# A channel MLP's block products computed as seven instead of eight in the second layer

## The chip, the cores and the metric

The kernel runs on one core of one Trainium2 chip. The metric is the device time of one execution in microseconds (us); the median of three runs is given, with their lowest and highest. Times in the sections below come from one profiled execution.

## What is computed

Two layers of a diffusion trunk over 640 tokens: 512 latent ones and 128 context ones, of width 1024. Each layer mixes the tokens by three branches, projects the merged result, and ends with a squared-ReLU MLP of hidden width 4096, which is where the change acts. Everything is held in fp32.

```python
def layer(x, cond, lp, lam_init, cached):
    ...
    merged = g_a * (y_a @ lp['w_o_gla']) + g_b * (y_b @ lp['w_o_mla']) + g_c * (y_c @ lp['w_o_diff'])
    x = x + gt1 * (merged @ lp['w_out'])

    h2 = rms_norm(x, lp['g_norm2']) * (1 + sc2) + sh2
    x = x + gt2 * (jnp.square(jax.nn.relu(h2 @ lp['w_mlp1'])) @ lp['w_mlp2'])
    return x, new_state
```

Layers are numbered 0 and 1. "Layer one" is the second and last.

## The kernel before

**Products.** TensorE multiplies 128x128 weight tiles with 256 or 384 token columns, since the tokens are cut into HALVES of 256 and 384. Every fp32 operand is split into a high part, which ScalarE makes by a cast (L98, or L1329 for the hidden values), and a low part, which is the operand minus its high part and comes from VectorE (L100, L1331). A product is then three matmuls for each 128 rows of the contraction: high by high, high by low, low by high (mm3, L105 to L107). At the start of the kernel and in parts of layer 0 GpSimd makes the low parts of weights in VectorE's place.

**The MLP.** The hidden width is cut into four blocks j of 1024. A block has 8 weight tiles of w1 (up) and then 8 of w2 (down); each tile is 128 columns of output by 1024 of contraction, 512 KB. load_w fetches a tile in one DMA issued by SyncE, casts it and subtracts, in turn with buffers of tag w (wraw 2, whi and wlo 3 each) and of tag x (xraw 1, xhi and xlo 3 each). A tile costs TensorE 8 x 3 matmuls of 256 columns and 8 x 3 of 384. An up tile's result goes through ReLU and square on ScalarE (L1328, L1329); GpSimd squares the ReLU once more in fp32 (L1330) for the low part. A down tile's result is scaled and added into the residual x by VectorE, straight from PSUM (L1279).

**Ahead of it.** out_proj (L1289) multiplies the merged rows by w_out for both token halves, adds them into x, and gathers sums of squares on ScalarE (L282) and VectorE (L283). norm (L330 to L334) turns x into the MLP's input: statistics matmuls (L301), a chain of twelve small VectorE instructions for 1/sqrt (L127 to L134), a broadcast matmul (L305), and then for each of the 8 tiles of 128 rows a product (VectorE, "nt"), the high part with the shift added (ScalarE, "hh") and the low part (VectorE, "hl"). The first half is normed while out_proj still works on the second.

**Order.** Each engine has its own queue, worked off in order. A list scheduler in the framework orders the instructions of each queue; a buffer's next use waits until its last reader is done. DMAs of weights are issued by SyncE in order.

**Rope tables.** The rope table (384 KB) is loaded once at the start and stays in SBUF; tables(l) at L338 works out per-layer tables from it on GpSimd (L363, L371).

## Time and profile before

| | |
|---|---|
| median of three runs | 2612.6 us (2611.7 to 2614.41) |
| the profiled execution's own time | 2612.42 us |
| its span, first to last instruction | 2610.6 us |
| first matmul of layer 1's MLP | 2155.79 us |
| last matmul of all | 2606.22 us |

The span starts at the first instruction. Busy time is the time in which an engine executes; a wait is put down to what ended it. "Granted clock" 1.00 is TensorE's higher level of 2.4 GHz and 0.50 its lower of 1.2 GHz.

### The profile page before, as it was taken

The page shows a single profiled execution, that of the slowest core. Times are in us where ns is not written, and L with a number is a line of the kernel's source. Part 1 is how long each engine was busy: PE and PEld are TensorE (multiplying, and loading weights), DVE is VectorE, ACT ScalarE, POOL GpSimd, SP SyncE. Part 2 cuts the span into 40 slices and gives each one's busy share as a digit, 9 for nine tenths or more (in the row PEclk, how much of TensorE's full clock was granted, in tenths as well). Part 3 has the DMA queues.
Part 4 walks back from the last instruction along what each step waited for, and adds up shares of the span by engine and source line. Part 5 has one row for each costly group of instructions (what it writes and reads, how often), then busy time and mean ns, then how long its engine had stood idle before and what let it go on. Part 6 is the DMA issues. An engine that isn't in the chain of part 4 may idle for free.

```text
span 2610.6 us, 45018 instructions
## 1 busy us (share of the span) xinstructions
PE 2511.1 (96%) x17616; PEld 2428.3 (93%) x17616; DVE 1595.3 (61%) x3613; ACT 1195.1 (46%) x2358; POOL 407.6 (16%) x550
## 2 busy tenths in 40 slices
PE   7899999899899999999989999998999999999999
PEld 3898999898899999999989888998989999999999
DVE  5787666578564776666655776666764455333332
ACT  4376687466333423132335777765652334132230
POOL 1321233010020111020221222511002001011010
PEclk9999999999999999999989999999999999999999
DMA  7411111413653244444421111123225332222221
GB/s 264 166 52 66 54 51 56 122 52 126 214 162 133 88 162 153 153 150 149 137 72 54 47 58 64 43 74 94 82 89 181 134 108 89 73 73 79 75 74 49
DMA packets 107572, 269.22 MB, mean 103 GB/s; under 512 B 12064, under 2 KB 42016, under 8 KB 105824
## 3 DMA queue, kind: packets, MB, share of 16 engines
q1 hardware_dynamic: 107360, 266.34, 30.6%
q8 instruction: 139, 2.28, 0.4%
q14 instruction: 73, 0.60, 0.1%
HBM read 235.86 MB, written 30.44 MB: 102 GB/s over the span
## 4 chain that ended last, share of the span: by engine, by line
PE 78%; DVE 12%; ACT 5%; DMA 3%; issue 2%; POOL 1%; SPq 0%; DVEq 0%; ACTq 0%; POOLq 0%
PE g L105 19%; PE g L106 19%; PE g L107 19%; PE go L534 2%; PE f L105 2%; PE f L106 2%; PE f L107 2%; DVE mjunk L212 1%; DVE sm_m L784 1%; PE y L1056 1%; PE g L852 1%; DMA modwe<-wmod 1%; DVE wlo L100 1%; PE gt L107 1%; PE gt L105 1%
## 5 line engine op out<-in xcount | busy, mean ns | idle before, releaser
L98 ACT CAST whi<-wraw 128x1024 fp32r<-128x1024 f32 (+2 forms) x236 | 220.2, 933 | 446.1 <-PE g L106 385.9
L100 DVE TENSOR_TENSOR wlo<-wraw,whi 128x1024 fp32r<-128x1024 f32 (+3 forms) x230 | 252.3, 1097 | 228.6 <-ACT whi L98 221.5
L105 PE MATMUL g<-hh,whi 128*128 128x256 f32 (+1 forms) x992 | 311.9, 314 | 6.5 <-DVE gla_t L633 4.8
L107 PE MATMUL g<-hh,wlo 128*128 128x256 f32 (+1 forms) x992 | 310.5, 313 | 3.3 <-DVE wlo L100 3.3
L106 PE MATMUL g<-hl,whi 128*128 128x256 f32 (+1 forms) x992 | 309.8, 312 | 0.0
L1330 POOL TENSOR_TENSOR relu<-relu 128x256 f32<-128x256 f32 (+1 forms) x128 | 110.8, 866 | 940.8 <-ACT uh L1329 937.9
L1279 DVE SCALAR_TENSOR_TENSOR x<-g,moda,x 128x256 f32<-128x256 f32 (+1 forms) x240 | 98.1, 435 | 219.6 <-PE g L107 219.4
L98 ACT CAST xhi<-xraw 128x1024 fp32r<-128x1024 f32 (+1 forms) x80 | 83.4, 1043 | 281.4 <-PE g L106 257.9
L105 PEld LDWEIGHTS g<-hh,whi 128*128 128x128 f32 x992 | 189.9, 191 | 7.9 <-issue 5.2
L107 PEld LDWEIGHTS g<-hh,wlo 128*128 128x128 f32 x992 | 189.3, 191 | 3.5 <-DVE wlo L100 3.5
L106 PEld LDWEIGHTS g<-hl,whi 128*128 128x128 f32 x992 | 189.9, 191 | 0.3 <-DVE hl L334 0.3
L212 DVE CUSTOM_DVE_ANT_0 mjunk<-modwm,condb 128x1024 bf16<-128x1024 f32 x112 | 140.1, 1250 | 45.5 <-DMA modwm<-wmod 45.1
L107 PE MATMUL g<-hh,xlo 128*128 128x384 f32 (+1 forms) x544 | 167.7, 308 | 0.0
L105 PE MATMUL g<-hh,xhi 128*128 128x384 f32 (+1 forms) x544 | 167.6, 308 | 0.0
L106 PE MATMUL g<-hl,xhi 128*128 128x384 f32 (+1 forms) x544 | 167.5, 308 | 0.0
L106 PE MATMUL g<-ul,whi 128*128 128x384 f32 (+1 forms) x512 | 158.1, 309 | 1.6 <-DVE ul L1331 1.6
L107 PE MATMUL g<-uh,wlo 128*128 128x384 f32 (+1 forms) x512 | 158.3, 309 | 0.0
L105 PE MATMUL g<-uh,whi 128*128 128x384 f32 (+1 forms) x512 | 158.2, 309 | 0.0
L107 PE MATMUL g<-uh,xlo 128*128 128x384 f32 (+1 forms) x512 | 157.8, 308 | 0.0
L106 PE MATMUL g<-ul,xhi 128*128 128x384 f32 (+1 forms) x512 | 157.8, 308 | 0.0
L105 PE MATMUL g<-uh,xhi 128*128 128x384 f32 (+1 forms) x512 | 157.7, 308 | 0.0
L105 PE MATMUL f<-hh,whi 128*128 128x256 f32 (+1 forms) x448 | 140.5, 314 | 4.6 <-ACT gth L1217 4.5
(451 smaller groups left out, 7689.6 us busy)
## 6 DMA issues: line engine op xcount, KB each, us to landing
wraw<-w SPq DMA_DIRECT2D x64, 512.0 KB, 3.5
xraw<-w SPq DMA_DIRECT2D x64, 512.0 KB, 3.5
wraw<-wfm SPq DMA_DIRECT2D x62, 512.0 KB, 3.6
modwm<-wmod SPq DMA_DIRECT2D x56, 512.0 KB, 3.5
wraw<-wn SPq DMA_DIRECT2D x36, 512.0 KB, 3.8
wraw<-wo SPq DMA_DIRECT2D x48, 256.0 KB, 3.0
mraw<-wmods SPq DMA_DIRECT2D x8, 1024.0 KB, 9.1
...
```

The source lines that it names most:

```text
L98: nc.scalar.copy(hi, raw)
L100: eng.tensor_tensor(lo, raw, hi.bitcast(F32), op=ALU.subtract)
L105: mm(out, wh, xh, start=first, stop=False)
L106: mm(out, wh, xl, start=False, stop=False)
L107: mm(out, wl, xh, start=False, stop=last)
L212: nc.vector.tensor_tensor_reduce(out=junk, in0=w, in1=self.condb[:, s], scale=0.5, scalar=0.0, op0=ALU.mult, op1=ALU.add, accum_out=self.m ...
L534: nc.tensor.matmul(p[:, hd], km[:, hd, cs], qm[:, hd, cs])
L784: nc.vector.tensor_reduce(out=nm, in_=sc, axis=ax, op=ALU.max, negate=True)
L852: nc.tensor.transpose(p[:, i * 256 + j * 128:i * 256 + j * 128 + 128], pts[j][:, (k0 + i) * 128:(k0 + i) * 128 + 128], self.ident)
L1056: nc.tensor.matmul(py[:, 2 * qp + j], aT[kt][:, j * 128:j * 128 + 128], vs[kt][:, vcs], start=(kt == 0), stop=(kt == 4))
L1279: self.nc.vector.scalar_tensor_tensor(dst[:, p0:p1], p[:, p0 - c0:p1 - c0], self.moda[l][:, kind * 8 + m, s:s + 1], src[:, p0:p1], op0=ALU ...
L1330: nc.gpsimd.tensor_tensor(r[:, :n], r[:, :n], r[:, :n], op=ALU.mult)
```

## The change

In layer 1 alone (FAST) the MLP's products are formed by Strassen's idea. Two weight tiles of rows i and i + 4, two halves of the contraction (512 each) and two halves of the tokens (now 320 and 320, EQ) make a 2 by 2 by 2 block product, which is written as seven products (numbered 1 to 7) of sums of blocks. A **job** is such a pair of tiles: 4 up and 4 down jobs for each j, 32 in all; the text calls them U0 to U3 and D0 to D3. A product is 4 x 3 matmuls of 320 columns.

weight() makes a job's seven weight operands out of two raw rows of 512 KB (buffers wraw, still two): products 1 and 2 take a block as it is, in ScalarE's cast and VectorE's subtraction; the operand of 4 has its low part from GpSimd, which then forms two sums of blocks in place; VectorE forms two more, and operands 5, 6, 7 and 3 follow from these. gather() adds the products up into four result blocks on VectorE, reading PSUM. The MLP's inputs need sums too (T1 to T4): norm_quarters and sums() make them from the normed x, up_on from the hidden values, on VectorE and GpSimd, each split again into high and low. down_on scales on ScalarE and adds into x on GpSimd; the last block does both on VectorE.

START, STEADY and DOWN are the orders of (job, products). In START and DOWN, rows 0 of two jobs are loaded for their products 1 and 2 and are loaded again for the other five, since wrow keeps two rows. out_proj of layer 1 also takes the halves of 320. Beside this the rope table is loaded anew in each layer, by tables(l), into a pool that other tiles share, where it stood in SBUF for good before.

```diff
@@ constants
+EQ = ((0, 320), (320, 640))
+EQ_PARTS = (((0, 320, 0),), ((320, 512, 0), (512, 640, 1)))
+FAST = (1,)
+REST = (6, 7, 4, 5, 3)
+START = [(0, (1, 2)), (1, (1, 2)), (2, (1,)), (0, REST), (1, REST), (2, (2,) + REST), (3, (1, 2) + REST)]
+STEADY = [(i, (1, 2) + REST) for i in range(4)]
+DOWN = [(4, (1,)), (5, (1,)), (4, (2,)), (5, (2,)), (4, REST), (5, REST), (6, (1, 2) + REST), (7, (1, 2) + REST)]
 LEVELS = (1, 2, 4, 8, 16, 32, 64)
 MASKED = LEVELS[1:6]
 VEC = 32
...
@@ TAGS
+    "hx": ("hx", 12), "hf": ("nrm", 16), "rope": ("gth", 1),
+    "b11": ("mlp", 2), "b12": ("mlp", 2), "b21": ("mlp", 1), "b22": ("mlp", 1),
...
-        self.rope = C([128, 4, 192], "rope")
-        nc.sync.dma_start(self.rope, a["rope"])
...
@@ class Net
+    def norm_quarters(self, l, xs, half):
+        nc = self.nc
+        c0, c1 = self.hv[half]
+        bc = self.bc[half]
+        for i in range(4):
+            s = self.hq[i]
+            for k, o in ((i, "b12" if half else "b11"), (i + 4, "b22" if half else "b21")):
+                t = self.S([128, 384], F32, "nt")
+                s.f[o] = self.S([128, 320], F32, "hf")
+                for p0, p1, m in EQ_PARTS[half]:
+                    q = slice(p0 - c0, p1 - c0)
+                    nc.vector.scalar_tensor_tensor(
+                        t[:, q], bc[:, q], self.moda[l][:, 32 + k, m:m + 1], xs[k][:, p0:p1], op0=ALU.mult, op1=ALU.mult)
+                    nc.scalar.activation(s.f[o][:, q], t[:, q], AF.Identity, bias=self.moda[l][:, 24 + k, m:m + 1])
+                if o != "b12":
+                    self.two(s.f[o], s[o.upper()])
+        for late in (0, 1) if half else ():
+            for s in self.hq:
+                self.sums(s, late)
+    def two(self, src, o, eng=None):
+        nc = self.nc
+        nc.scalar.copy(o[:, 0], src)
+        (eng or nc.vector).tensor_tensor(o[:, 1], src, o[:, 0].bitcast(F32), op=ALU.subtract)
+    def sums(self, s, late):
+        nc, f = self.nc, s.f
+        sub = lambda eng, o, x, y: eng.tensor_tensor(f[o], f[x], f[y], op=ALU.subtract)
+        if not late:
+            sub(nc.vector, "b11", "b12", "b11")
+            self.two(f["b11"], s["T1"])
+            sub(nc.gpsimd, "b12", "b22", "b12")
+            sub(nc.vector, "b22", "b22", "b11")
+            self.two(f["b22"], s["T2"])
+        else:
+            sub(nc.vector, "b21", "b21", "b22")
+            self.two(f["b12"], s["T3"], nc.gpsimd)
+            self.two(f["b21"], s["T4"], nc.gpsimd)
+    def wrow(self, job, r):
+        for key, t in self.raws:
+            if key == (job["key"], r):
+                return t
+        t = self.S([128, 8, 128], F32, "wraw")
+        self.nc.sync.dma_start(t, job["src"][r])
+        self.raws = self.raws[-1:] + [((job["key"], r), t)]
+        return t
+    def wop(self):
+        self.turn += 1
+        return self.S([128, 2, 4, 128], F32R, ("whi", "wlo")[self.turn % 2])
+    def weight(self, job, n):
+        nc = self.nc
+        if n in (1, 2):
+            o = self.wop()
+            self.two(self.quart(job, 0, n - 1), o)
+            return o
+        if n not in self.wops:
+            if not self.raws or self.raws[-1][0] != (job["key"], 0):
+                self.raws = []
+            q = [[self.quart(job, r, c) for c in range(2)] for r in range(2)]
+            op = lambda eng, o, x, y, f: eng.tensor_tensor(o, x, y, op=f)
+            def put(m, src, eng=None):
+                self.wops[m] = self.wop()
+                self.two(src, self.wops[m], eng)
+            put(4, q[1][1], nc.gpsimd)
+            op(nc.gpsimd, q[1][1], q[1][0], q[1][1], ALU.add)
+            op(nc.gpsimd, q[1][0], q[0][0], q[1][0], ALU.subtract)
+            op(nc.vector, q[0][0], q[1][1], q[0][0], ALU.subtract)
+            op(nc.vector, q[0][1], q[0][1], q[0][0], ALU.subtract)
+            for m, src in ((5, q[1][1]), (6, q[0][0]), (7, q[1][0]), (3, q[0][1])):
+                put(m, src)
+            self.raws = []
+        return self.wops.pop(n)
+    def quart(self, job, r, c):
+        return self.wrow(job, r)[:, c * 4:c * 4 + 4]
+    def product(self, st, n):
+        w = self.weight(st, n)
+        bs = [s[("B11", "B21", "B22", "T4", "T1", "T2", "T3")[n - 1]] for s in st["right"]]
+        out = self.P([128, 512], "n" if n == 1 and st["hold"] else "g")[:, 0:320]
+        for k in range(4):
+            self.mm3(out, w[:, 0, k], w[:, 1, k], bs[k][:, 0], bs[k][:, 1], k == 0, k == 3)
+        if n == 1 and st["hold"]:
+            st["first"] = out
+            return
+        if n == 2 and st["hold"]:
+            self.gather(st, 1, st["first"])
+        self.gather(st, n, out)
+    def gather(self, st, n, p):
+        nc = self.nc
+        f = st["out"].f if "out" in st else st["f"]
+        for o in {1: ("b12",), 2: ("b11",), 7: ("b22",), 4: ("b21",)}.get(n, ()):
+            f[o] = self.S([128, 320], F32, o)
+        add = lambda o, x: nc.vector.tensor_tensor(f[o], f[x], p, op=ALU.add)
+        if n == 1:
+            nc.scalar.copy(f["b12"], p)
+        elif n == 2:
+            add("b11", "b12")
+            st["on"](st, "b11")
+        elif n == 6:
+            add("b12", "b12")
+        elif n == 7:
+            add("b22", "b12")
+        elif n == 4:
+            add("b21", "b22")
+            st["on"](st, "b21")
+        elif n == 5:
+            add("b12", "b12")
+            add("b22", "b22")
+            st["on"](st, "b22")
+        elif n == 3:
+            add("b12", "b12")
+            st["on"](st, "b12")
+    def up_on(self, st, o):
+        nc, s = self.nc, st["out"]
+        f = s.f
+        nc.scalar.activation(f[o], f[o], AF.Relu)
+        nc.scalar.activation(f[o], f[o], AF.Square)
+        if o == "b12":
+            for n in ("T1", "T2", "T3", "T4"):
+                s.new(n)
+            self.sums(s, 0)
+            self.sums(s, 1)
+        else:
+            s.new(o.upper())
+            self.two(f[o], s[o.upper()])
+    def down_on(self, st, o):
+        row, half = int(o[1]) - 1, int(o[2]) - 1
+        m = st["m"] + 4 * row
+        x = st["xs"][m]
+        c0, c1 = EQ[half]
+        t = st["f"][o]
+        for p0, p1, s in EQ_PARTS[half]:
+            g, tp = self.moda[st["l"]][:, 40 + m, s:s + 1], t[:, p0 - c0:p1 - c0]
+            if st["last"]:
+                self.nc.vector.scalar_tensor_tensor(x[:, p0:p1], tp, g, x[:, p0:p1], op0=ALU.mult, op1=ALU.add)
+            else:
+                self.nc.scalar.mul(tp, tp, g)
+        if st["last"]:
+            self.nc.sync.dma_start(self.a["o_x"][:, m, c0:c1], x[:, c0:c1])
+        else:
+            self.nc.gpsimd.tensor_tensor(x[:, c0:c1], x[:, c0:c1], t, op=ALU.add)
+    def mlp_fast(self, l, xs):
+        a = self.a
+        self.raws, self.wops = [], {}
+        hid = [Slots(self, f"u{i}") for i in range(4)]
+        for j in range(4):
+            jobs = [{"key": (1, j, i), "src": (a["w1"][l, j * 8 + i], a["w1"][l, j * 8 + i + 4]), "right": self.hq,
+                     "out": hid[i], "on": self.up_on, "hold": (i, j) == (2, 0)} for i in range(4)]
+            jobs += [{"key": (2, j, m), "src": (a["w2"][l, j, m], a["w2"][l, j, m + 4]), "right": hid, "on": self.down_on,
+                      "hold": False, "f": {}, "l": l, "m": m, "xs": xs, "last": j == 3} for m in range(4)]
+            for i, ns in (STEADY if j else START) + DOWN:
+                for n in ns:
+                    self.product(jobs[i], n)
...
     def tables(self, l):
         nc = self.nc
+        self.rope = self.S([128, 4, 192], F32, "rope")
+        nc.sync.dma_start(self.rope, self.a["rope"])
         row = self.S([128, ROW], F32, "rowb")
...
-        self.norm_begin()
+        fast = l in FAST
+        if fast:
+            self.hq = [Slots(self, "hh") for i in range(4)]
+            for s in self.hq:
+                for n, s.tag in (("T1", "hh"), ("T2", "hl"), ("B11", "hh"), ("B21", "hl")):
+                    s.new(n)
...
             if (m, i) == (8 - SKEW[0], 1):
-                self.norm(l, 1, xs, 0)
+                if fast:
+                    self.norm_scale(0)
+                    self.norm_quarters(l, xs, 0)
+                else:
+                    self.norm(l, 1, xs, 0)
...
+        if l in FAST:
+            self.hv, self.parts = EQ, EQ_PARTS
...
+        if l in FAST:
+            w2.close()
+            w2.enter_context(self.pool("hx", side="right"))
+            for s in self.hq:
+                s.tag = "hx"
+                for n in ("B22", "T3", "T4"):
+                    s.new(n)
+            self.norm_scale(1)
+            self.norm_quarters(l, xs, 1)
+            nrm.close()
+            with self.pool("mlp"):
+                self.mlp_fast(l, xs)
+            return xp, nrm, pm, w2
...
```

Two places in VectorE's queue, as they stood and as they stand.

VectorE in layer 1's down phase, before: the low parts of two weight tiles (wlo, xlo) and between them the residual's update out of PSUM (g).

```order
L100 TENSOR_TENSOR xlo_28393<-xraw_28390,xhi_28392 128x1024
L1279 SCALAR_TENSOR_TENSOR x_24462<-g_28074,moda1_92,x_24462 128x256
L1279 SCALAR_TENSOR_TENSOR x_24462<-g_28100,moda1_92,x_24462 128x256
L1279 SCALAR_TENSOR_TENSOR x_24462<-g_28100,moda1_92,x_24462 128x128
L100 TENSOR_TENSOR wlo_28461<-wraw_28458,whi_28460 128x1024
L1279 SCALAR_TENSOR_TENSOR x_24463<-g_28133,moda1_92,x_24463 128x256
```

None of these rows is left: a low part of 1024 columns becomes low parts of 512, and the update of x goes to ScalarE and GpSimd (in the last block j it stays on VectorE).

VectorE at such a place after, for jobs D2 and D3 of a block j. wraw_27549 is row 0 of D3 and wraw_27588 its row 1; whi and wlo are both names of operand tiles; b12_27424 and b22_27494 are result blocks of D2, b11_27584 and b12_27566 of D3, and g a product in PSUM.

```order
L428 TENSOR_TENSOR wraw_27549<-wraw_27588,wraw_27549 128x512
L386 TENSOR_TENSOR wlo_27597<-wraw_27588,wlo_27597 128x512
L467 TENSOR_TENSOR b12_27424<-b12_27424,g_27513 128x320
L467 TENSOR_TENSOR b22_27494<-b22_27494,g_27513 128x320
L428 TENSOR_TENSOR wraw_27549<-wraw_27549 128x512
L467 TENSOR_TENSOR b12_27424<-b12_27424,g_27531 128x320
L386 TENSOR_TENSOR whi_27600<-wraw_27549,whi_27600 128x512
L386 TENSOR_TENSOR wlo_27603<-wraw_27588,wlo_27603 128x512
L386 TENSOR_TENSOR whi_27606<-wraw_27549,whi_27606 128x512
L467 TENSOR_TENSOR b11_27584<-b12_27566,g_27571 128x320
L467 TENSOR_TENSOR b12_27566<-b12_27566,g_27609 128x320
```

The two sums of D3's weights (L428), the four low parts that follow from them, and the gathering of D2's products 5 (twice) and 3 (L467) now stand in one row; the two sums stand behind GpSimd's in-place ones on the same buffers.

VectorE at the entry of layer 1's MLP, before: the norm of the second token half (nt, hl) for its last tiles of x.

```order
L334 SCALAR_TENSOR_TENSOR hl_24483<-nt_25113,moda1_92,hh_24482 128x128
L330 SCALAR_TENSOR_TENSOR nt_25127<-n_25056,moda1_92,x_24463 128x256
L334 SCALAR_TENSOR_TENSOR hl_24485<-nt_25120,moda1_92,hh_24484 128x256
L334 SCALAR_TENSOR_TENSOR hl_24485<-nt_25120,moda1_92,hh_24484 128x128
L334 SCALAR_TENSOR_TENSOR hl_24487<-nt_25127,moda1_92,hh_24486 128x256
L330 SCALAR_TENSOR_TENSOR nt_25127<-n_25056,moda1_92,x_24463 128x128
L1331 TENSOR_TENSOR ul_25183<-relu_25209,uh_25182 128x256
```

Before, the last nt and its low part ended the norm, and the low parts of hidden values (ul) followed at once.

The same place after: the end of the second half's norm (nt), then sums of the normed blocks (hf) and their low parts (hh, hl, hx), and at the end the first job's weight sums (L428).

```order
L391 TENSOR_TENSOR hf_24942<-hf_24942,hf_25119 128x320
L386 TENSOR_TENSOR hl_24484<-hf_25161,hl_24484 128x320
L391 TENSOR_TENSOR hf_24954<-hf_24954,hf_25133 128x320
L391 TENSOR_TENSOR hf_24966<-hf_24966,hf_25147 128x320
L391 TENSOR_TENSOR hf_24978<-hf_24978,hf_25161 128x320
L428 TENSOR_TENSOR wraw_25324<-wraw_25326,wraw_25324 128x512
L386 TENSOR_TENSOR wlo_25335<-wraw_25326,wlo_25335 128x512
L428 TENSOR_TENSOR wraw_25324<-wraw_25324 128x512
L386 TENSOR_TENSOR whi_25338<-wraw_25324,whi_25338 128x512
```

Behind the norm's last nt there are now 22 such instructions on blocks of 320 columns, and behind these the operand of U0's product 6 (whi_25338), the first product that needs a sum.

## Rows read from the trace of the kernel before

**Rows 1.** The page: busy us of each engine, its share of the span, instructions.

```profile
PE 2511.1 (96%) x17616; PEld 2428.3 (93%) x17616; DVE 1595.3 (61%) x3613; ACT 1195.1 (46%) x2358; POOL 407.6 (16%) x550
```

**Rows 2.** Stretches: length, each engine's busy time and instructions, granted clock, DMA.

```profile
2150.00:2200.00 50.00, 50.00 (x340) 49.87 (x339) 34.89 (x82) 26.78 (x54) 8.98 (x11) 1.00 0.26 82
...
2300.00:2350.00 50.00, 50.00 (x345) 50.00 (x345) 16.84 (x26) 14.22 (x23) 6.82 (x9) 1.00 0.23 75
```

**Rows 3.** TensorE's timeline in layer 1's MLP: start, duration, form.

```profile
2155.79 0.29 PE L105 MATMUL g<-hh,whi 128*128 128x256 f32 x1
2155.91 0.28 PE L106 MATMUL g<-hl,whi 128*128 128x256 f32 x1
...
2300.55 0.34 PE L105 MATMUL g<-hh,whi 128*128 128x384 f32 x1
2300.73 0.34 PE L106 MATMUL g<-hl,whi 128*128 128x384 f32 x1
...
2606.22 0.34 PE L107 MATMUL g<-uh,xlo 128*128 128x384 f32 x1
```

**Rows 4.** VectorE by form, 2080 to 2611: count, busy us, mean ns, idle before.

```profile
L1279 DVE SCALAR_TENSOR_TENSOR x<-g,moda,x 128x256 f32<-128x256 f32 x80 | 38.7, 483 | 156.1 <-PE g L107 156.0
L1331 DVE TENSOR_TENSOR ul<-relu,uh 128x384 fp32r<-128x384 f32 x32 | 17.9, 560 | 23.0 <-POOL relu L1330 23.0
L1331 DVE TENSOR_TENSOR ul<-relu,uh 128x256 fp32r<-128x256 f32 x32 | 13.8, 437 | 31.6 <-POOL relu L1330 31.6
...
L100 DVE TENSOR_TENSOR wlo<-wraw,whi 128x512 fp32r<-128x512 f32 x1 | 0.7, 693 | 4.8 <-ACT whi L98 4.8
```

**Rows 5.** ScalarE by form, same stretch.

```profile
L1329 ACT ACTIVATE uh<-relu 128x384 fp32r<-128x384 f32 x32 | 16.8, 526 | 1.0
...
L98 ACT CAST whi<-wraw 128x512 fp32r<-128x512 f32 x1 | 0.6, 620 | 3.6 <-PE g L106 3.6
```

**Rows 6.** GpSimd on the timeline: adds of two SBUF inputs, 256 and 384 columns.

```profile
2009.51 0.74 POOL L1266 TENSOR_TENSOR x<-x,th 128x256 f32<-128x256 f32 x1 [0.78 <-DVE th L1264]
...
2028.33 1.02 POOL L1266 TENSOR_TENSOR x<-x,th 128x384 f32<-128x384 f32 x1 [1.28 <-DVE th L1264]
```

**Rows 7.** VectorE and GpSimd side by side, both with two SBUF inputs.

```profile
1340.70 0.56 DVE L283 TENSOR_TENSOR sqacc<-sqacc,sqt 128x384 f32<-128x384 f32 x1
...
1342.17 2.26 DVE L283 TENSOR_TENSOR sqacc<-sqacc,sqt 128x384 f32<-128x384 f32 x1 [0.65 <-ACT sqt L282]
...
1341.68 2.34 POOL L100 TENSOR_TENSOR xlo<-xraw,xhi 128x1024 fp32r<-128x1024 f32 x1 [3.89 <-ACT xhi L98]
```

**Rows 8.** DMA issues: bytes, median us from issue to landing.

```profile
wraw<-w SPq DMA_DIRECT2D x64, 512.0 KB, 3.5
```

**Rows 9.** Timeline at the entry of layer 1's MLP, VectorE and TensorE.

```profile
2144.17 0.16 DVE L127 TENSOR_SCALAR rq_v<-n 128x2 f32<-128x2 f32 x1 [0.70 <-PE n L301]
...
2146.34 0.16 DVE L134 SCALAR_TENSOR_TENSOR nr<-rq_t,nr 128x2 f32<-128x2 f32 x1
2147.30 1.27 DVE L330 SCALAR_TENSOR_TENSOR nt<-n,moda,x 128x256 f32<-128x256 f32 x3 [0.81 <-PE n L305]
...
2159.02 0.72 PE L301 MATMUL n<-one,sqacc 128*128 128x1 f32 x6
```

**Rows 10.** TensorE's waits by releaser: us in total, times, longest.

```profile
PE g L105 <- ACT whi L98: 8.3, 2, 4.2
...
PE g L105 <- ACT yh L138: 7.4, 1, 7.4
...
PE g L106 <- POOL xlo L100: 4.6, 2, 4.4
```

**Rows 11.** The stretches around the first two of those waits (347 and 686 us).

```profile
351.00:355.00 4.00, 3.60 (x19) 3.60 (x20) 3.87 (x5) 3.79 (x7) 3.64 (x6) 0.58 0.18 38
...
689.00:693.00 4.00, 0.00 (x0) 0.00 (x0) 1.38 (x3) 0.55 (x1) 0.00 (x0) 0.50 0.98 334
...
696.00:699.00 3.00, 3.00 (x13) 3.00 (x13) 0.49 (x1) 1.16 (x2) 0.00 (x0) 0.50 0.86 277
```

More of the change, by code (lines that the diff above doesn't have):

```diff
@@ L73, with __init__, new @@
 ROW = 448
+class Slots(dict):
+    def __init__(self, net, tag):
+        self.net, self.tag, self.f = net, tag, {}
+    def new(self, n):
+        self[n] = self.net.S([128, 2, 320], F32R, self.tag if self.tag[0] == "h" else self.tag + n)
 class Net:
@@ L81, in S @@
     def S(self, shape, dt, name):
-        pool, bufs = TAGS[name] if name in TAGS else ("small", 2)
+        if name[0] == "u" and name[1] in "0123":
+            pool, bufs = "mlp", 1
+        else:
+            pool, bufs = TAGS[name] if name in TAGS else ("small", 2)
         return self.pools[pool].tile(list(shape), dt, name=name, tag=name, bufs=bufs)
@@ L275, in stat_add @@
         nc = self.nc
-        c0, c1 = HALVES[half]
+        c0, c1 = self.hv[half]
         if self.sq_first[half]:
@@ L295, in norm_scale @@
         nc = self.nc
-        c0, c1 = HALVES[half]
-        nt = (c1 - c0) // 128
+        c0, c1 = self.hv[half]
+        os = list(range(0, c1 - c0 - 128, 128)) + [c1 - c0 - 128]
+        nt = len(os)
         bc = self.bc[half] = self.P([128, 512], "n")
         st = bc[:, 384:384 + nt]
-        for i in range(nt):
-            nc.tensor.matmul(st[:, i:i + 1], self.sq[:, c0 + i * 128:c0 + i * 128 + 128], self.one)
+        for i, o in enumerate(os):
+            nc.tensor.matmul(st[:, i:i + 1], self.sq[:, c0 + o:c0 + o + 128], self.one)
         r = self.S([128, nt], F32, f"nr{nt}")
         self.rsqrt(r, st, 1.0 / D, nt)
-        for i in range(nt):
-            nc.tensor.matmul(bc[:, i * 128:i * 128 + 128], r[:, i:i + 1].to_broadcast([128, 128]), self.ident)
+        for i, o in enumerate(os):
+            nc.tensor.matmul(bc[:, o:o + 128], r[:, i:i + 1].to_broadcast([128, 128]), self.ident)
     def norm_scale_all(self):
@@ L335, in norm_apply @@
                     self.h[k][1][:, p0:p1], tp, sh, self.h[k][0][:, p0:p1].bitcast(F32), op0=ALU.add, op1=ALU.subtract)
+    def norm_quarters(self, l, xs, half):
+        nc = self.nc
+        c0, c1 = self.hv[half]
+        bc = self.bc[half]
[14 more added lines that the diff above has]
+                self.sums(s, late)
@@ L1275, in add_res @@
     def add_res(self, l, kind, m, half, p, src, dst):
-        c0 = HALVES[half][0]
-        for p0, p1, s in PARTS[half]:
+        c0 = self.hv[half][0]
+        for p0, p1, s in self.parts[half]:
             self.nc.vector.scalar_tensor_tensor(
@@ L1294, in out_proj @@
         wts = {}
-        self.norm_begin()
+        fast = l in FAST
[4 more added lines that the diff above has]
+                    s.new(n)
+        else:
+            self.norm_begin()
         for m, i in self.order(0, SKEW[0]):
             if (m, i) == (8 - SKEW[0], 1):
-                self.norm(l, 1, xs, 0)
+                if fast:
+                    self.norm_scale(0)
+                    self.norm_quarters(l, xs, 0)
+                else:
+                    self.norm(l, 1, xs, 0)
             if m not in wts:
@@ L1308, in out_proj @@
                 self.mod_some(OUT_MODS[m])
-        self.norm(l, 1, xs, 1)
+        if not fast:
+            self.norm(l, 1, xs, 1)
         return xs
@@ L1378, in run @@
         self.pools, self.open, self.turn, self.pool_lo = {}, set(), 0, True
+        self.hv, self.parts = HALVES, PARTS
         with ExitStack() as top:
```

10 lines of the change are left out of this document (5 added, 5 removed).

## The prediction, made before the changed kernel had run

> **What bounds the kernel now.** I read the share of busy time first: TensorE is busy for 96% of the span [rows 1]. A share is an average over stages, so I then read the changed stage in stretches of 50 us. From 2150 to 2600 TensorE is busy for 50.00 of each 50 us at a granted clock of 1.00, while VectorE needs 17 to 35, ScalarE 14 to 27 and GpSimd 7 to 9 [rows 2]. Nobody waits for the other engines there; this stage costs what its matmuls cost. On the timeline two matmuls of 256 columns start 0.12 us apart and two of 384 columns 0.17 to 0.18 apart [rows 3]; over long rows of them the steps are 0.118 and 0.1725. The stage holds 4 x 16 tiles x 24 = 1536 of each: 1536 x (0.118 + 0.1725) = 446 us, and from the first matmul at 2155.79 to the last at 2606.22 [rows 3] it is 450, with the norm's matmuls in it.
>
> **What TensorE saves.** The change leaves 32 jobs x 7 products x 12 = 2688 matmuls of 320 columns. Midway between the two steps one costs 0.1453, so a product takes 1.74 us, a job 12.2, and all 390.7. That is 55.7 us less, if TensorE still sets the pace. Everything below asks whether it does: the same change multiplies the work of the engines that had been idle, and chains it.
>
> **The loop that prepares a job's weights.** wraw keeps two rows, so the next job's rows are fetched only when this job's last low part (operand 3) has read its row. Then, in the order of the queues: the DMA, 3.5 us [rows 8]; ScalarE's cast of 512 columns, 0.62 [rows 5]; on GpSimd, which has no row of 512 columns, a low part, a sum and a difference. Its adds took 0.74 for 256 columns and 1.02 for 384 [rows 6], so 1.30 for 512 on the same line, and 0.88 for 320: 3 x 1.30. Then VectorE's sum, 0.69 [rows 4], and behind it in its row one more sum and the low parts of 5, 6, 7 and 3: 5 x 0.66. With 0.7 for hand-offs a turn is at least 3.5 + 0.62 + 3.9 + 0.69 + 3.3 + 0.7 = **12.7 us**, against TensorE's 12.2. So TensorE loses the lead, by little.
>
> The turn is longer where the row holds more. For D2 the order puts one gather of the job before (0.5 for 320 columns) among the sums: 13.0. For D3 it puts three, and the two sums lie further apart: 14.2 (the second excerpt of the change). Mean 13.6; 8 such jobs, (13.6 - 12.2) x 8 = **+11**.
>
> D0 and D1 come as a pair whose rows 0 are fetched once for products 1 and 2 and again for the rest: 6.1 us (DMA, two casts and low parts) and two turns of 12.2 to 12.7 make 30.5 in place of 24.4. Four pairs, **+24**.
>
> Up jobs also split and sum hidden values. VectorE works on 8 x 0.69 of weights, 8 two-input instructions of 320 columns (0.50, between 0.437 and 0.560 [rows 4]) and 7 gathers. Here a conflict counts. VectorE's sum of 384 columns, 0.56 alone, took 2.26 when it met a GpSimd subtraction of 2.34 that had started 0.5 us before: it ended with it [rows 7]. Instructions of the two engines with two SBUF inputs so run one after the other. In an up job that is 8 x 0.69 + 8 x 0.50 on VectorE and 3 x 1.30 + 3 x 0.88 on GpSimd, 16.1 us in all; in a down job 5.5 and 3.9 + 4 x 0.88, 12.9. Walking each row of the order by hand, with operands of the job before as they arrive, I get 14.0, 14.5, 17.7 and 14.8 for U0 to U3, and take 15.3. ScalarE's ReLU and square (0.53 for 384 columns [rows 5]) lie in that chain too. 14 single up jobs: (15.3 - 12.2) x 14 = **+43**; U0 and U1 of the first block are in the entry. From both sides a turn lies between 12.7 and the sum of 16.1 with a gather's wait, 16.5.
>
> The Trainium skill's page "SBUF — State Buffer", section "Who interferes with whom", says that an instruction of VectorE with two SBUF inputs and one of GpSimd that reads SBUF take a shared port in turn, whoever starts first holding it to the end. The trace agrees (2.26 beside 2.34 [rows 7]). Without it an up job would go by VectorE's own 12.6 us and the chain, 13.5, the entry would cost 20, and the sum would be 2639.
>
> **The entry.** Before, half a norm hid behind products of the other half. Now START has 5 products, 8.7 us, that need no sum. The second half's statistics matmuls stand in TensorE's row 33 matmuls (4.8 us) after out_proj's end; the chain for 1/sqrt and the broadcast takes 2147.30 - 2144.17 = 3.1 [rows 9], and with the last squares of out_proj the first nt starts about 9.0 after that end. Before it, too, TensorE passed the statistics in the middle of other products [rows 9]. Then 16 products nt, 4 low parts, 20 more sums and low parts of 320 columns (0.50) and four of 512 lead to the operand of product 6. Unhindered that is at 29, with GpSimd's 12 instructions of 0.88 in between up to 39. So TensorE waits 20 to 30; I take **+22**, near the lower end, since most of GpSimd's come behind the rows that matter. U1's five later products (8.7 us) then wait for a turn of 14 of their own: **+5**.
>
> **The clock.** Waits of 4.2 and 7.4 us [rows 10] were followed by stretches at the lower level: granted clock 0.58 from 351 to 355, and 0.50 from 689, within the wait, until 699 [rows 11]. The first is 3.4 us at half, 1.7 of work lost. After the entry I expect the longer case, and after the pairs' waits the short one: **+5**. Between single jobs the waits are 1 to 3 us, and I count nothing (see D).
>
> **The rest.** Where GpSimd's subtraction delayed TensorE by 4.4 us [rows 10] in layer 0, the order now has that subtraction before the tables, whose rope DMA comes later: **-2** (0 to -5). In layer 1 the reload delays tables that are first read far later; cost 0, hidden by layer 1's input products. out_proj with 320 halves and the tail (the last update and its DMA) keep their cost, within 1.
>
> **Sum.** -55.7 + 11 + 24 + 43 + 22 + 5 + 5 - 2 = +52. From the execution's own 2612.4 (the median is 2612.6, the same) that gives 2665.
>
> **Rivals.**
> A, the forecast: the weights' loop sets the pace, 2625 to 2695.
> B: TensorE sets it in all jobs, since fetches run ahead of what I take the buffers to allow; only the entry, clock and start count: -55.7 + 22 + 3 - 2 = -33, 2580, faster. It decides if a turn is under 12.2 us. The chain of 12.7 speaks against it; each of its links has a row but GpSimd's.
> C: single jobs run at the bare chain of 12.7, with the gathers hidden, and a pair takes 27: -55.7 + 22 x 0.5 + 4 x 2.6 + 20 + 4 (U1) + 3 - 2 = -9, 2603; 2590 to 2622.
> D: the waits inside each job also bring the clock down. 1.7 us for each of 22 single jobs and for two waits of each pair add 51: 2716. For it: [rows 11] after a wait of 4.2. Against it: the turns' waits are 1 to 3 us. The Trainium skill's "TensorE: Matmul & The Clock Gate", section "HAM oscillation", describes a loop that waited for a DMA in every tile and ran slowed in every one, which is D; no run here shows it for waits this short.
> That the change leaves TensorE's work as it was is out: the order holds 2688 matmuls for 3072.
>
> **How the numbers follow.** A 0.60, B 0.09, C 0.14, D 0.17. C splits into 0.08 faster, 0.04 within 0.2% (5 us, about what a measurement can tell from no change) and 0.02 slower. So faster 0.17, same 0.04, slower 0.79. The range leaves out B, some half of C and the top of D: 2600 to 2716. Inside it the uncertain size is the turn: one us on each of 32 jobs is 32 us. The time is A's.
>
> **What would show it.** Right: TensorE busy for 38 to 45 of 50 us between 2200 and 2600, waiting for VectorE's low parts (operand 1 and operand 6) and ScalarE's casts; a gap of some 20 us near 2165; wraw's DMAs issued once per 13 to 16 us in pairs. Wrong: TensorE without waits there (B), DMAs of rows issued while the job before is still being prepared (B, C), a granted clock under 0.9 throughout (D), GpSimd's 512 columns under 1 us or the two engines overlapping (C).

## The result: slower by 5.5%, and the profile after

The changed kernel took 2756.73 us in the median of four runs (2752.91 to 2757.09), the kernel before 2612.15; the ratio is 1.0547 (1.0534 to 1.056). The direction was forecast and the size was not: +52 was expected, +145 came, 41 us beyond the top of the range.

The page of the changed kernel, busy time by engine:

```profile
PE 2514.6 (91%) x17236; PEld 2417.2 (88%) x17236; DVE 1825.7 (66%) x4029; ACT 1352.7 (49%) x2762; POOL 588.1 (21%) x690
```

No engine is full. The next two lines are one stretch of 400 us inside layer 1's MLP, before and after (length, busy time and count of PE, PEld, DVE, ACT, POOL, granted clock, DMA):

```profile
2200.00:2600.00 400.00, 400.00 (x2738) 400.00 (x2737) 128.44 (x198) 100.66 (x159) 40.80 (x53) 1.00 0.22 72
```

```profile
2200.00:2600.00 400.00, 314.17 (x1866) 303.25 (x1865) 252.59 (x429) 195.81 (x415) 167.72 (x147) 0.88 0.21 66
```

TensorE was busy for all of it before and is busy for 79% of it now, at a mean clock of 0.88. VectorE's busy time has doubled and GpSimd's is four times what it was, and they are busy for 63% and 42% of the stretch. That is how a chain looks: each engine waits for another in turn. TensorE's waits from 2140 on, by what ended them (us in total, times, longest), have no counterpart before, where the stage had none:

```profile
PE g L129 <- ACT wlo L385: 64.2, 17, 8.5
PE g L129 <- ACT whi L385: 41.1, 11, 18.2
PE g L131 <- DVE whi L386: 15.9, 13, 2.1
PE g L131 <- DVE wlo L386: 13.7, 11, 2.4
```

All four are operands of weights (whi and wlo are both names of operand tiles; L385 is the cast, L386 the low part). They add to 135 us. The MLP took from 2162.87 to the end of its last matmul at 2751, 588 us against 450; the other 7 us were lost before it began.

```profile
2162.72 0.31 PE L131 MATMUL g<-mh,xlo 128*128 128x320 f32 x1
2162.87 0.30 PE L129 MATMUL g<-hh,wlo 128*128 128x320 f32 x1
2163.01 0.31 PE L130 MATMUL g<-hh,wlo 128*128 128x320 f32 x1
...
2750.90 0.31 PE L131 MATMUL g<-u3B,whi 128*128 128x320 f32 x1
```

The step of a 320-column matmul is 0.145 to 0.146 us where TensorE does not wait, as worked out from [rows 3]. The saving of 55 us was there to be had, and none of it arrived.

**The turn, measured.** I call a turn the time from the end of one job's last low part (operand 3) to that of the next. These ends are read from VectorE's timeline. In means:

| | forecast | measured | jobs | missed |
|---|---|---|---|---|
| single down job (D2, D3) | 13.6 | 16.4 | 8 | 22 |
| pair D0 and D1 | 30.5 | 37.7 | 4 | 29 |
| single up job | 15.3 | 17.7 | 14 | 34 |
| start of the kernel to layer 1's out_proj | -2 | +6 | | 8 |

These sum to 93 us, and the forecast fell short by 92. Job by job the single up turns were 16.4, 19.8, 17.9 and 17.0 for U0 to U3, where 14.0, 14.5, 17.7 and 14.8 had been walked: U1 is furthest off, U2 nearly right. What follows asks what a turn consists of.

**One turn in full.** D3 of the third block: D2's last low part ends at 2586.0, D3's at 2603.6, a turn of 17.6 where 14.2 was walked. ScalarE's timeline first (start, duration, form, idle before and what ended it):

```profile
2588.71 0.62 ACT L385 CAST whi<-wraw 128x512 fp32r<-128x512 f32 x1 [1.71 <-DMA wraw<-w]
2589.23 0.61 ACT L385 CAST wlo<-wraw 128x512 fp32r<-128x512 f32 x1
2591.58 0.62 ACT L385 CAST whi<-wraw 128x512 fp32r<-128x512 f32 x1 [1.74 <-PE g L131]
```

The third cast is that of operand 4. It starts 5.6 us after the last low part, not 3.5. The two rows are fetched one over the other, and its own row landed 5.2 us after that low part; the last 0.4 is a wait for a slot, which a product of the job before still read. Over all single turns of this trace that cast starts 4.9 us after the last low part in D2 and D3 and 4.3 in up jobs (means), and in only 3 of the 32 jobs was it the slot that came last. Then GpSimd, and then VectorE:

```profile
2592.28 1.60 POOL L386 TENSOR_TENSOR whi<-wraw,whi 128x512 fp32r<-128x512 f32 x1 [4.34 <-ACT whi L385]
2593.96 2.68 POOL L428 TENSOR_TENSOR wraw<-wraw 128x512 f32<-128x512 f32 x2
2596.59 0.89 POOL L519 TENSOR_TENSOR x<-x,b 128x320 f32<-128x320 f32 x1
2600.29 0.86 POOL L519 TENSOR_TENSOR x<-x,b 128x320 f32<-128x320 f32 x1 [2.81 <-ACT b L515]
2601.45 0.99 POOL L519 TENSOR_TENSOR x<-x,b 128x320 f32<-128x320 f32 x1 [0.29 <-ACT b L515]
```

```profile
2593.35 0.49 DVE L467 TENSOR_TENSOR b<-b,g 128x320 f32<-128x320 f32 x1 [0.62 <-PE g L131]
2596.68 1.36 DVE L428 TENSOR_TENSOR wraw<-wraw 128x512 f32<-128x512 f32 x1 [2.84 <-POOL wraw L428]
2597.96 0.68 DVE L386 TENSOR_TENSOR wlo<-wraw,wlo 128x512 fp32r<-128x512 f32 x1
2598.56 0.87 DVE L467 TENSOR_TENSOR b<-b,g 128x320 f32<-128x320 f32 x2
2599.36 0.68 DVE L428 TENSOR_TENSOR wraw<-wraw 128x512 f32<-128x512 f32 x1
2599.96 0.47 DVE L467 TENSOR_TENSOR b<-b,g 128x320 f32<-128x320 f32 x1
2600.36 1.35 DVE L386 TENSOR_TENSOR whi<-wraw,whi 128x512 fp32r<-128x512 f32 x1
2601.63 1.36 DVE L386 TENSOR_TENSOR wlo<-wraw,wlo 128x512 fp32r<-128x512 f32 x1
2602.91 0.68 DVE L386 TENSOR_TENSOR whi<-wraw,whi 128x512 fp32r<-128x512 f32 x1
```

GpSimd's two sums of 512 columns took 1.34 each; 1.30 had been estimated from [rows 6]. But GpSimd starts its next instruction, an addition into x, at 2596.59, 0.09 us before VectorE's first sum, and that sum takes 1.36 for 0.68. The same happens to the low parts of 6 and 7 beside the additions at 2600.29 and 2601.45. The gather (L467) at 2593.35, with one operand in PSUM, took 0.49 in the middle of GpSimd's low part of 1.60. This is the conflict of [rows 7], three times in one turn and each time on the chain: 2.0 us.

### The profile page after: what moved, and what is told of

Same layout as the page of the kernel before. It is cut to its first block, busy times and chain, and to the rows that moved or that the text cites. A ratio compares the mean times of both kernels' runs of the same rounds, so it can differ in the third digit from the quotient of the medians.

```text
span 2755.2 us, 45416 instructions
## 1 busy us (share of the span) xinstructions
PE 2514.6 (91%) x17236; PEld 2417.2 (88%) x17236; DVE 1825.7 (66%) x4029; ACT 1352.7 (49%) x2762; POOL 588.1 (21%) x690
## 4 chain that ended last, share of the span: by engine, by line
PE 60%; DVE 17%; ACT 7%; DMA 6%; POOL 5%; issue 5%; SPq 0%; POOLq 0%; ACTq 0%; DVEq 0%
PE g L129 13%; PE g L131 13%; PE g L130 13%; DMA wraw<-w 4%; POOL wraw L428 3%; PE f L129 2%; PE go L733 2%; PE f L131 2%; PE f L130 2%; DVE wlo L386 1%; DVE wraw L428 1%; PE y L1255 1%; DVE sm_m L983 1%; DVE whi L386 1%; DMA modwe<-wmod 1%
## 5 line engine op out<-in xcount | busy, mean ns | idle before, releaser
L131 PE MATMUL g<-hh,wlo 128*128 128x384 f32 (+2 forms) x800 | 251.4, 314 | 6.9 <-DVE wlo L124 6.9
L129 PE MATMUL g<-hh,whi 128*128 128x384 f32 (+2 forms) x796 | 251.2, 316 | 6.4 <-DVE gla_t L832 4.7
L130 PE MATMUL g<-hl,whi 128*128 128x384 f32 (+2 forms) x804 | 253.4, 315 | 0.0
L234 DVE CUSTOM_DVE_ANT_0 mjunk<-modwm,condb 128x1024 bf16<-128x1024 f32 x112 | 142.4, 1271 | 38.9 <-DMA modwm<-wmod 38.6
L467 DVE TENSOR_TENSOR b<-b,g 128x320 f32<-128x320 f32 x224 | 104.8, 481 | 65.2 <-PE g L131 62.2
L131 PE MATMUL f<-hh,wlo 128*128 128x256 f32 (+1 forms) x448 | 140.0, 312 | 0.2
L130 PE MATMUL f<-hl,whi 128*128 128x256 f32 (+1 forms) x448 | 139.9, 312 | 0.0
L385 ACT CAST whi<-wraw 128x512 fp32r<-128x512 f32 x112 | 69.1, 617 | 115.5 <-DMA wraw<-w 47.2
L983 DVE TENSOR_REDUCE sm_m<-sc 128x1 f32<-128x640 f32 x128 | 104.1, 818 | 18.6 <-PE sc L1218 14.2
L385 ACT CAST wlo<-wraw 128x512 fp32r<-128x512 f32 x112 | 68.8, 617 | 93.1 <-DMA wraw<-w 33.9
L129 PE MATMUL g<-whi,hh 128*128 128x256 f32 (+1 forms) x360 | 105.1, 292 | 8.3 <-ACT whi L122 8.3
```

The lines of the kernel that those rows point to most:

```text
L129: mm(out, wh, xh, start=first, stop=False)
L130: mm(out, wh, xl, start=False, stop=False)
L131: mm(out, wl, xh, start=False, stop=last)
L234: nc.vector.tensor_tensor_reduce(out=junk, in0=w, in1=self.condb[:, s], scale=0.5, scalar=0.0, op0=ALU.mult, op1=ALU.add, accum_out=self.m ...
L385: nc.scalar.copy(o[:, 0], src)
L467: add = lambda o, x: nc.vector.tensor_tensor(f[o], f[x], p, op=ALU.add)
```

## The experiments

Theory A is the prediction's: the chain of fetch, cast, sums and low parts sets the turn. B: the sum of what VectorE and GpSimd do with two SBUF inputs, one after the other, sets it. C: the lower clock after each wait is what costs. P is a finer form of A: those conflicts count that hit the chain itself. Each time in the table is one run; the four runs of the changed kernel lay within 4.2 us. Means of turns in us, as above (the pair is two jobs); the kernel after has 17.7, 37.7, 16.4.

| | us | up | pair | down |
|---|---|---|---|---|
| e2 half-row buffers | 2690.2 | 16.4 | 29.3 | 15.4 |
| e3 weight sums on VectorE | 2704.5 | 16.5 | 35.2 | 13.9 |
| e4 no pair | 2737.1 | 17.7 | 33.7 | 16.0 |
| e5 e2 with operand 4 early | 2676.6 | 15.2 | 33.3 | 13.6 |
| e6 e2 and e3 | 2671.3 | 15.6 | 30.6 | 13.5 |
| e7 product 2 twice | 2751.0 | 17.8 | 38.6 | 15.9 |
| e8 e5 and e3 | 2645.4 | 14.9 | 29.7 | 12.5 |
| e9 no additions into x | 2736.6 | 17.7 | 36.0 | 14.9 |
| e10 hidden sums on VectorE | 2760.2 | 17.7 | 41.5 | 15.8 |
| e11 e8, no pair | 2643.1 | 14.8 | 30.1 | 12.0 |
| e13 no hidden differences | 2726.4 | 16.5 | 35.1 | 16.4 |

**Does TensorE have time to spare?** e7 gives it back just the work that the change saves.

```diff
-        for k in range(4):
+        for k in list(range(4)) * (1 + (n == 2)):
             self.mm3(out, w[:, 0, k], w[:, 1, k], bs[k][:, 0], bs[k][:, 1], k == 0, k == 3)
```

> The changed kernel with product 2 of each job computed twice in a row into the same place: 12 matmuls more a job, 32 x 1.74 = 56 us of TensorE's work, which is just what the seven products save. A and B (another engine's work sets the pace, TensorE waits 3 us and more in each job): the work goes into the waits, 2757 to 2775 us. If TensorE set the pace: 2810. C (the lower clock after the waits is what costs): with shorter waits less of the stage runs at the lower clock (142 us of it now), so the time falls, 2735 or less.

Measured: 2751.0, 5.7 us less than the kernel after and 6 under the range of A and B, with 56 us more of matmuls. The same stretch of 400 us in e7:

```profile
2200.00:2600.00 400.00, 347.43 (x2148) 337.98 (x2149) 251.36 (x428) 194.63 (x415) 167.13 (x146) 0.93 0.21 69
```

TensorE is busy for 33 us more at a clock of 0.93 in place of 0.88; VectorE, ScalarE and GpSimd did the same amount in the same time. TensorE sets no pace here. It also takes C out as the main cause: the clock rose and the turns stayed as they were. What C may still be worth lies in the 5.7 us.

**Is the fetch in the turn?** e2 uses the same 8 KB a partition as four half-rows.

```diff
+FETCH = ((1, 1), (0, 0), (1, 0), (0, 1))
...
-        t = self.S([128, 8, 128], F32, "wraw")
-        self.nc.sync.dma_start(t, job["src"][r])
-        self.raws = self.raws[-1:] + [((job["key"], r), t)]
+        self.rown = (self.rown + 1) % 4
+        t = self.rows[self.rown // 2][:, self.rown % 2 * 4:self.rown % 2 * 4 + 4]
+        self.nc.sync.dma_start(t, job["src"][r][:, c * 4:c * 4 + 4])
+        self.raws = self.raws[-3:] + [(key, t)]
...
+        if n == 1 and job["whole"]:
+            for r, c in FETCH:
+                self.quart(job, r, c)
```

> The two row buffers of weights are used as four half-row buffers, each fetched again as soon as its own last reader is done; the order of fetches follows the order of releases. Same memory, same matmuls and sums. A: the DMA leaves the turn in part (the first half-row can start some 5 us before the last low part), 3 to 3.5 us off each of 32 jobs: 2645 to 2665 us. B: the sum of the two engines' two-input work stays, 16.1 us an up job and 12.9 a down job; measured turns of 16 to 20 and 15 to 17.6 fall by 2 on the mean: 2690. C: the waits only get shorter and the granted clock stays near 0.89; not below 2720.

Measured: 2690.2, 67 us less: the number of B, but not its turns. B's sums were 16.1 for up jobs, which took 16.4, and 12.9 for down jobs, which took 15.4. ScalarE's timeline shows why (the third and fourth rows are the casts of operands 2 and 4):

```profile
2537.15 0.62 ACT L386 CAST whi<-wraw 128x512 fp32r<-128x512 f32 x1 [0.29 <-DMA wraw<-w]
2538.08 0.57 ACT L523 ACTIVATE b<-b,moda 128x320 f32<-128x320 f32 x1 [0.32 <-DVE b L475]
2540.99 0.62 ACT L386 CAST wlo<-wraw 128x512 fp32r<-128x512 f32 x1 [2.34 <-DMA wraw<-w]
2541.51 0.61 ACT L386 CAST whi<-wraw 128x512 fp32r<-128x512 f32 x1
```

Operand 4's half-row is fetched first, but its cast stands in ScalarE's row behind that of operand 2, whose half-row comes last. The fetch had left the buffers and come back through a queue. e5 prepares operand 4 and GpSimd's two sums, which are now in sums4(), before operand 2:

```diff
...
+            if n == 1 and job["whole"]:
+                self.sums4(job, [[self.quart(job, r, c) for c in range(2)] for r in range(2)])
```

> As e2_quarter, with operand 4 and GpSimd's two sums prepared before operand 2. In e2 ScalarE's cast for operand 4 stood behind the cast for operand 2, whose half-row comes last, so that the fetch was still inside the turn, and every turn took 15.2 to 15.4 us. A (the chain of fetch, casts and sums sets the turn): all turns fall by some 2.5 us, up jobs too; 2690 - 32 x 2.5 = 2610, 2600 to 2625 us. B (the port that VectorE and GpSimd share sets it): down jobs fall to 13, up jobs stay at 15 to 16; 2645 to 2660. C (the clock): 2680 or more.

Measured: 2676.6, a number that neither theory had. A wanted 2.5 us off every turn. Down jobs lost 1.9 (15.4 to 13.6) and up jobs 1.2 (16.4 to 15.2), so single turns came out nearer to B's 13 and 15 to 16 than to A's. The pairs took 4 us each more (29.3 to 33.3), which neither had foreseen.

**Is GpSimd's share in the chain?** In e3 the low part and the two sums that GpSimd makes of a job's weights go to VectorE (`nc.gpsimd` to `nc.vector` in three calls of weight()).

> The three weight instructions of each job that GpSimd makes (a low part and two sums of 512 columns) are made by VectorE; row buffers as in the changed kernel. A: the chain inside the turn gets shorter by 3 x (1.4 - 0.65) and by the 0.7 that VectorE's next sum waits behind GpSimd's following instruction: 2.8 to 3 us a job, 2660 to 2670 us. B: of the 16.1 us of an up job 3.9 us leave and 2.0 come back, 1.9 less: 2695. C: not below 2720.

Measured: 2704.5, 10 above B's number and 35 above A's; down turns 2.5 us shorter, up turns 1.2. On e2's buffers:

> As e2_quarter, with the three weight instructions of GpSimd on VectorE, as in e3_nopool. A: 3 x (1.3 - 0.65) + 0.7 = 2.7 us leave each turn of 15.3; 2690 - 86 = 2604, to 2620. B: in up jobs VectorE's own work (11 x 0.6 + 8 x 0.41 + 7 x 0.40 = 12.7) and GpSimd's 2.6 still add to 15.3, down jobs fall to TensorE's 12.2: 2690 - 16 x 3 = 2642. C: 2680 or more.

Measured: 2671.3, 29 above B's number and 51 above the top of A's; 1.9 and 0.8 us shorter than e2. A wanted 2.7 to 3 a turn: twice down jobs gave most of it, and up jobs less than half. With everything together:

> e5 and e6 together: half-row buffers, operand 4 and the first two sums before operand 2, all sums of weights on VectorE. A: the chain is shorter than TensorE's 12.2 us a job, which then sets the pace; entry and start remain: 2590 to 2605. B: up jobs stay at VectorE's and GpSimd's 15.3, down jobs at 12.2 to 13: 2635 to 2650.

Measured: 2645.4, in B's range. Down jobs run at TensorE's pace (12.5), up jobs do not (14.9). The stretch in e8:

```profile
2200.00:2600.00 400.00, 364.83 (x2367) 356.54 (x2365) 356.69 (x632) 245.26 (x529) 109.87 (x96) 0.97 0.27 85
```

VectorE is busy for 357 of 400 us. Here, it seems, a load has taken the place of the chain: B's 15.3 for up jobs is 0.4 us off. But that is a mean; by job they run from 12.3 (U0) to 17.6 (U2), and no run changes VectorE's load by itself.

**The pair.** e4 runs the down jobs one after the other:

```diff
-DOWN = [(4, (1,)), (5, (1,)), (4, (2,)), (5, (2,)), (4, REST), (5, REST), (6, (1, 2) + REST), (7, (1, 2) + REST)]
+DOWN = [(i, (1, 2) + REST) for i in range(4, 8)]
```

> The four down jobs of a block follow one after the other, each with rows fetched once, in place of the pair D0 and D1 whose rows 0 are fetched twice. A: a pair took 38 us in the trace after (22.5 to 23.3 and 13.6 to 16.0), two single down jobs take 33; against that, D0's products 1 and 2 no longer run ahead of the last up job's sums. 4 x 5 = 20 us less at best, 2737 to 2750 us. B: the same work on both engines, within 10 us of 2757. C: fewer long waits, up to 10 us less.

Measured: 2737.1, A's lower end; D0 and D1 take 33.7 in place of 37.7. The double fetch costs 4 us a pair as long as the chain rules. In e8's kernel the same edit:

> e8_quarter_early_nopool with the down jobs one after the other (as e4_plain_down). In e8 VectorE is busy for 45 of 50 us and sets the pace; a pair still took 28 to 31 us against 24 for two single down jobs, so 4 x 5 = 20 us less by theory A: 2625 to 2630. If VectorE's load alone sets the pace, the pair's second fetch costs nothing, and it stays at 2640 to 2645. Either way slower than before.

Measured: 2643.1, 2.3 us under e8 and the number expected if VectorE's load rules: the second fetch is hidden here. It is the best of the versions with seven products, still 31 us slower than before.

**The conflicts on the chain.** e9 leaves out GpSimd's additions into x in three of the four blocks (last lines of down_on()).

> The changed kernel without GpSimd's additions into the residual in the down jobs of blocks j = 0 to 2 (this part of the result is left out); the last block is as it was. P (in the turn VectorE's sums and low parts wait for the port while GpSimd adds into x: 1.36 us in place of 0.68, three times in the turn of D2.3): the 6 single down turns of these blocks fall from 16.4 to 14.4, the three pairs from 38 to 35; 6 x 2 + 3 x 3 = 21 us less, 2736 us; up jobs and the last block as they were. A (fetch, casts and the order of the queues alone make the turn, the conflicts lie in its slack): within 5 us of 2757.

Measured: 2736.6. Down turns of those blocks fell from 16.4 to 14.5, their pairs from 38.3 to 36.0, up turns stayed at 17.7: P's numbers. In D3's row nothing meets GpSimd any longer:

```profile
2581.51 0.69 DVE L386 TENSOR_TENSOR whi<-wraw,whi 128x512 fp32r<-128x512 f32 x1
2582.11 0.69 DVE L386 TENSOR_TENSOR wlo<-wraw,wlo 128x512 fp32r<-128x512 f32 x1
2583.39 0.69 DVE L386 TENSOR_TENSOR whi<-wraw,whi 128x512 fp32r<-128x512 f32 x1 [0.60 <-ACT whi L385]
```

So of the 2.8 us by which a down turn was too short in the forecast, 1.9 are additions of 0.88 us each, on an engine that is idle for more than half of the stretch. (e9 takes them out of GpSimd's queue too; the three conflicts of D3's turn alone make 2.0.) The Trainium skill's "SBUF — State Buffer", section "Who interferes with whom", states as a rule that the later of two such instructions fully blocks; the row of 1.36 beside 0.89, and 0.69 without, agree.

**Up jobs.** In e10 the hidden blocks' sum and low parts, and those of the normed x at the entry, go from GpSimd to VectorE (`nc.gpsimd` to `nc.vector` in sums()).

> The changed kernel with the sum and the two low parts of 320 columns that GpSimd makes of the hidden values in each up job, and of the normed x at the entry, on VectorE. P: 3 x (0.88 to 1.05) of GpSimd holding the port leave an up job, and 3 x 0.41 come to VectorE: 1.5 us off each of 16 up jobs, and at the entry 12 x (1.0 - 0.4) = 7 less; 2757 - 30 = 2727. A: VectorE's row only gets longer, 1 us more an up job: 2760 to 2775.

Measured: 2760.2, A's number, and P fails here. But A has that number by luck: up turns stayed at 17.7 where it wanted 1 us more, the pairs took 15 us more in all, and U1 of the first block was done 6 us earlier. Either the conflicts of up jobs lie in slack, or they cost as much as three more instructions on VectorE; e10 does not tell these apart. The changed kernel's ScalarE in U1 of the third block, between the low part of 7 (ends 2491.7) and that of 3 (ends 2497.4), 5.8 us for an expected 0.7:

```profile
2492.25 0.46 ACT L385 CAST u0T<-b 128x320 fp32r<-128x320 f32 x1
2493.37 0.46 ACT L385 CAST u0T<-b 128x320 fp32r<-128x320 f32 x1 [0.66 <-POOL b L391]
2493.73 0.62 ACT L385 CAST whi<-wraw 128x512 fp32r<-128x512 f32 x1
```

The last is the cast of operand 3, whose row the next fetch waits for. It stands behind a cast of a hidden sum of U0, which waits for GpSimd's difference, which waits for VectorE's, which waits for U0's last product. That is 2 of the 5.8 us. The cast ends at 2494.35, and VectorE's queue holds the low part (the last row) back for 1.7 us more:

```profile
2494.18 1.16 DVE L391 TENSOR_TENSOR b<-b,b 128x320 f32<-128x320 f32 x1
2495.27 0.47 DVE L467 TENSOR_TENSOR b<-b,g 128x320 f32<-128x320 f32 x1
2495.66 0.48 DVE L386 TENSOR_TENSOR u0T<-b,u0T 128x320 fp32r<-128x320 f32 x1
2496.07 1.37 DVE L386 TENSOR_TENSOR whi<-wraw,whi 128x512 fp32r<-128x512 f32 x1
```

This gap of 5.8 us stands in U1 of the last three blocks; in U0, U2 and U3 it is 0.6 to 2.1. e13 leaves the four differences out, and with them their places in both queues:

```diff
-            for n in ("T1", "T2", "T3", "T4"):
+            for n, b in (("T1", "b11"), ("T2", "b22"), ("T3", "b12"), ("T4", "b21")):
                 s.new(n)
-            self.sums(s, 0)
-            self.sums(s, 1)
+                self.two(f[b], s[n], nc.gpsimd if n in ("T3", "T4") else None)
```

> The changed kernel with the four differences of hidden blocks of each up job left out (three on VectorE, one on GpSimd, of 320 columns); T1 to T4 are split straight from the blocks, so casts, low parts and matmuls stay. H (in up jobs ScalarE's cast for operand 3, whose row the next fetch waits for, stands behind casts that wait for these differences): the 14 single up turns fall from 17.7 to about 15.3, 2757 - 34 = 2723, 2715 to 2732 us, and the gap between the low parts of 7 and 3 in U2.1 falls from 5.7 to under 3. L (only the engines' load counts): 3 x 0.4 of VectorE and 0.9 of GpSimd leave a job in which neither is full, 2745 to 2757.

Measured: 2726.4, inside the range of H, and the gap between the low parts of 7 and 3 fell from 5.8 to 2.7. But up turns fell to 16.5, half of the way to 15.3; 10 us of the 30 came in the pairs (37.7 to 35.1), which wait for the last up job's hidden blocks. The hidden differences are half of the up jobs' excess, mostly in U1 and U2 (2.4 and 2.1 us a turn); whether ScalarE's queue or VectorE's makes it, e13 does not tell. Of the other half the trace shows operand 4's cast, 0.8 us later than the 3.5 of the walk; no run tests what that costs.

**The 7 us before the MLP.** e1 switches the seven products off (`FAST = ()`) and keeps the rope table's fetch.

> The changed kernel with the seven products switched off in both layers; what is left of the change is the rope table loaded per layer. Theory A (the turn that prepares a job's weights sets the pace of layer 1's MLP, and the rest of the 144 us lies ahead of it): the trace after shows layer 1's first out_proj matmul 6.4 us later than before, so this kernel is 5 to 7 us slower than before, 2617 to 2620 us. The prediction's own step: 2 us faster, 2610. Theories B (the port that VectorE and GpSimd take in turn) and C (TensorE's clock after waits) say nothing else for it than A, since they act in the MLP only.

Measured: 2620.46 against 2613.55, ratio 1.0025 (1.0015 to 1.0034). The step "-2" had the wrong sign. TensorE's waits in the first 130 us, before and in e1:

```profile
PE g L106 <- POOL xlo L100: 4.6, 2, 4.4
PE g L233 <- ACT mrow L230: 4.2, 8, 0.7
PE g L107 <- DVE wlo L100: 3.3, 1, 3.3
```

```profile
PE g L255 <- ACT mrow L252: 7.2, 8, 2.4
PE g L131 <- DVE wlo L124: 7.0, 1, 7.0
...
PE g L130 <- POOL xlo L124: 2.0, 1, 2.0
```

The wait for GpSimd's low part did fall, by 2.6, as forecast. Two waits that the prediction did not look at grew by 6.7. To find what moved them, e12 only moves the one fetch of the kernel before into the first layer's tables, and e14 fetches in both layers, still into the lasting tile.

e14's edit is shown; e12 has `if not l:` ahead of the added fetch.

```diff
-        nc.sync.dma_start(self.rope, a["rope"])
...
+        nc.sync.dma_start(self.rope, self.a["rope"])
         row = self.S([128, ROW], F32, "rowb")
```

> The kernel before with one line moved: the rope table, loaded once as before and kept, is fetched in the first layer's tables and not with the constants. If the later fetch in layer 0 reorders the queues at the start and this is what e1_rope_only shows, 5 to 7 us slower than before, 2617 to 2620. If the fetch for layer 1 or the shared pool is what costs, within 2 us of before.

> The kernel before with its rope table, still in its own lasting tile, fetched in tables() of each layer: both fetches of the change without the pool that the change makes it share. If the second fetch is what e1_rope_only pays for, 2617 to 2620 us. If it is the shared pool (other small tiles now wait for its buffers and the queues at the start are ordered otherwise), 2612 to 2615, as e12_rope_late.

Measured: e12 2613.06 against 2612.29 (ratio 1.0003, 0.9994 to 1.0013), e14 2617.8 against 2612.65 (1.002, 1.001 to 1.003). So the second fetch brings most of the cost, though not where it stands: in e14's trace TensorE is level with before until 310 us and 4.8 behind from 380 on, a thousand us ahead of that fetch, while e1 loses its 4.2 before 160. The scheduler orders the queues otherwise in each of them. Which row of which queue costs, stays open.

## Why the prediction was wrong, point by point

- **What bounds the kernel, and TensorE's saving.** Right: 0.146 a matmul, and e7 shows that all of the saved work lies idle.
- **The mechanism.** Right: the preparation of the next job's weights, through two row buffers, outlasts TensorE's work. The chain's links stand in the trace in the order of the walk.
- **The size of the turn.** This is the step that failed, in "Mean 13.6", "I take 15.3" and "two turns of 12.2 to 12.7". The walk added each link at its undisturbed duration and kept the conflict of [rows 7] as a separate bound, "16.1 us in all", to be compared with the chain. They add instead where an instruction of the other engine falls on a link: 1.9 us of a down turn by e9. A fetch was priced at 3.5 us alone, where two overlap, and operand 4's cast began 4.9 us after the release in D2 and D3 and 4.3 in up jobs. Up jobs were short by 2.4, of which e13 finds 1.2 in the hidden differences; the rest is not shown by a run. Three slips of the working are small beside this. The row of 2.26 in [rows 7] ends 0.4 us after GpSimd's and not with it, which fits turns taken all the same; D2's 13.0 is 13.2 by its own terms; and the sum without the conflict is 2638, not 2639.
- **The pair.** Its two turns were taken at 12.2, and the rest, 6.1, was for the second fetch. In e4, which has no second fetch, the same two jobs take 33.7: about 16.8 each, with 4 left for the fetch. The turns were too short and the fetch too dear.
- **The bounds.** "Between 12.7 and 16.5" was taken for the range of a turn. 16.5 was a load, without the waits of a chain, and so bounds nothing from above: eight turns of 19 and more were measured, four of them of D0 with its second fetch and four of single up jobs.
- **The entry.** Right: operand 6 of the first job was forecast 30.7 us after out_proj's end (8.7 + 22); its low part ended at 2193.1, 30.3 after. TensorE's longest wait, 18.2, is this one, where 22 was forecast. U1's turn behind it took 16.8 for 14.
- **The clock.** Waits bring the clock down, as forecast, but far more of them: 0.88 is the mean clock of the stretch, and waits of single jobs were expected to bring none of it. But since TensorE sets no pace, it costs little (e7), and rival D, with the total nearest, owes that to luck: e7 shows little of its 51 us for the clock. The Trainium skill's "TensorE: Matmul & The Clock Gate", section "HAM oscillation", describes a loop that ran slowed after its wait in every tile; the row of 0.88 agrees that such waits slow the clock, and e7, 5.7 us faster at 0.93, shows little of the price that the Trainium skill puts on it.
- **The start.** Wrong in sign, -2 for +6 to 7: one wait that gets shorter was counted, and the order of the other queues was not.
